# An encoder block on one core: MLP operands made before the norm is known, weight sums added in DRAM, the input in half tiles, products in pairs

## The chip, the cores and the metric

The kernel runs on one core of a Trainium2 chip. The metric is the device time of one execution in microseconds; three runs of the kernel before were timed, and one further execution was profiled. Times below are in microseconds unless marked ns. PE is TensorE, DVE VectorE, ACT ScalarE, POOL GpSimd, SP the engine that issues most DMAs.

## The reference

One encoder layer over 1024 positions with 1024 features, in float32, cut to what matters here:

```python
h = rmsnorm(x, norm_mix_g);  z = h @ w_in                    # split: conv group, latent attention group
y_conv = bg * dwconv_centred(cg * xc, conv_w)                # 512 channels, width 3
y_mla  = mla_attention(q_nope, q_rope, k_nope, k_rope, v)    # 8 heads, softmax over 1024 keys
x = x + concatenate([y_conv, y_mla]) @ w_o

hf = rmsnorm(x, norm_ffn_g)
a = dwconv_centred(hf @ w_up, ffn_conv_w, ffn_conv_b)        # w_up: 1024 x 5632, conv over positions
g, u = split(a)
x = x + (silu(g) * u) @ w_down

gate = sigmoid(rmsnorm(x, ple_norm_g) @ w_ple_gate)
x = x + gate * (p @ w_ple_proj)
out = rmsnorm(x, final_norm_g)
```

`rmsnorm(x, g)` multiplies each position by 1 / sqrt(mean of squares + eps) and each feature by g. The factor of a position is the same for all features, so it can also be applied to the result of a matrix product.

## The kernel before

**Layout.** Activations lie with features on the 128 partitions and positions along the free dimension: eight tiles of 128 x 1024 for x. A float32 product is made from three products of split operands (`gemm`, line 139): each operand is kept as a rounded part ("h", type fp32r) and a remainder ("l"), made by an ACT copy and a DVE or POOL subtraction, and high x high, high x low and low x high are summed in PSUM. A matmul takes a 128 x 128 weight and a 128 x 512 operand.

**Stages in order.** Latent projections; convolution group in four rounds of three products (`unit_gemm`, the result of the third read from PSUM by DVE at line 414); preparation of keys, queries and values; attention; output projection (`out_mla`); the embedding products of p (`embed`) and the MLP's first half in 22 units; down projection in seven groups; gate and final norm.

**Attention.** The loop over `NT` = 64 blocks (8 heads x 8 blocks of 128 queries) issues `scores(i + 2)`, then `transposes(i)`, and every second time `values`. In `scores` DVE takes the maximum (line 511), ACT the exponential, and the scaling by the sum of each row is shared: ACT or DVE take 768 columns, POOL the last 256 (line 521). PE transposes the scaled block (line 534).

**The MLP's first half.** For each unit c (128 gate columns and 128 up columns) the product of the 2 x 2 blocked weight and the 2 x 2 blocked hf is made with seven block products in place of eight (`TERMS`, steps 1 to 7; `BANK` says which PSUM bank each adds into). Its stationary operands are the blocks a11, a12, a22 and four sums s1 to s4 of weight blocks; DVE makes the sums (lines 654 to 657) and the parts are split at lines 645 and 646. The moving operands are blocks b11, b21, b22 of hf and four differences t1 to t4; `up_moving` makes them once for all units: `scaled` (line 723) multiplies x by gain and norm factor, `diff` (line 726) makes differences and remainders, `put` (line 734) the rounded copies. `Unit.step(i)` issues one block product (12 matmuls), and `read` combines the results, then comes the convolution over positions (lines 261 to 263) and the store of the unit's result to `gud`.

**What sets the order.** PE's instructions keep the order of the program (`manual_schedule`). Between `dve_order.enter_context` and `dve_order.close` the same holds for DVE; elsewhere a planner orders the other engines' queues. The norm factors are made by `norm`: `norm_first` (16 small matmuls hung into a `gemm`, line 228), `norm_root` (DVE, lines 233 to 242), `norm_second` (16 small matmuls, line 253). The passage into the MLP runs

```python
    for d in range(6):
        if d == 2:
            norm_first()
        if d == 4:
            norm_second()
        embed(d)
        if d == 2:
            norm_root()
        if d == 4:
            up_moving(rs, lambda: pair.append(up_unit(1, weights1)))
```

and then the first two units' steps in pairs; units 2 to 21 follow one by one. POOL's own DMAs (line 891 loads x for the down projection) use descriptors that software writes; the program reserves `dynamic_dma_scratch_size=1024` bytes for them.

## Time and profile before

| | |
|---|---|
| median of 3 runs | 1356.63 (1356.61 to 1358.47) |
| profiled execution | 1356.78 |
| its span, first to last instruction | 1355.0 |
| mean granted TensorE clock | 0.989 |
| busy: PE, DVE, ACT, POOL | 1323.1, 1006.1, 597.3, 261.3 |
| matmuls | 6354 |
| DMA | 117.38 MB, mean 87 GB/s |

A row of a timeline gives start, duration, engine, line, operation, output <- input, size and count; in brackets stands the idle time before it and what ended that. A row of waits gives who waited for whom: total, times, longest. Rows of windows give the stretch, its length and each engine's busy time with the number of instructions, then the clock, the share of the DMA engines and GB/s.

### The profile page before, as it was taken

How to read it: one execution, taken by the hardware profiler on the slowest of the kernel's cores; microseconds unless marked ns; L12 is line 12 of the kernel's file. 1: busy time of each engine (PE TensorE's matmuls, PEld its weight loads, DVE VectorE, ACT ScalarE, POOL GpSimd, SP SyncE). 2: the span in 40 equal slices, each digit the busy share in tenths (PEclk: the TensorE clock that was granted, in tenths of full speed). 3: DMA queues.
4: the chain of work that ended last, by engine and by line, in shares of the span. 5: the costliest groups of instructions: out<-in, count | busy, mean ns of one | idle time of the engine just before them, and what ended most of it. 6: DMA issues, size and time to landing. Idle time of an engine off the chain costs nothing.

```text
span 1355.0 us, 16462 instructions
## 1 busy us (share of the span) xinstructions
PE 1323.1 (98%) x6354; PEld 1087.7 (80%) x6354; DVE 1006.1 (74%) x1336; ACT 597.3 (44%) x839; POOL 261.3 (19%) x222
## 2 busy tenths in 40 slices
PE   9999999999999999879999999999999999999997
PEld 7877788888888887658888888888877888888897
DVE  7478923799999957988887888888665555557786
ACT  5323422788888834543443444344331111125433
POOL 0286452455555510000000000000010000000000
PEclk9999999999999999979999999999999999999998
DMA  6201134200000254203222222222174222121123
GB/s 215 78 31 47 47 133 148 78 1 17 1 17 1 68 212 171 94 16 124 78 78 78 94 78 78 78 94 74 66 292 165 95 94 94 55 78 55 49 83 111
DMA packets 38894, 117.38 MB, mean 87 GB/s; under 512 B 4256, under 2 KB 9632, under 8 KB 38816
## 3 DMA queue, kind: packets, MB, share of 16 engines
q1 hardware_dynamic: 35824, 107.30, 22.7%
q10 hardware_dynamic: 1840, 4.83, 0.9%
q0 software_dynamic: 1152, 4.19, 0.8%
q8 instruction: 50, 0.82, 0.3%
q14 instruction: 28, 0.23, 0.0%
HBM read 88.00 MB, written 28.31 MB: 86 GB/s over the span
## 4 chain that ended last, share of the span: by engine, by line
PE 85%; DVE 9%; issue 2%; POOL 2%; ACT 1%; DMA 0%; POOLq 0%; SPq 0%; ACTq 0%
PE bk L139 56%; PE big L139 9%; PE small L139 4%; PE small L534 4%; PE small L547 2%; PE big L504 2%; PE big L508 2%; PE big L506 2%; PE small L546 2%; DVE tmp L163 1%; DVE xt L726 1%; DVE tmp L263 1%; DVE tmp L262 1%; DVE b L726 1%; DVE rbc L164 1%
## 5 line engine op out<-in xcount | busy, mean ns | idle before, releaser
L139 PE MATMUL bk<-gu,whi 128*128 128x512 f32 x704 | 194.7, 398 | 2.8 <-DVE x L904 2.2
L139 PE MATMUL bk<-b,wm 128*128 128x512 f32 x792 | 192.8, 396 | 1.7 <-DVE b L726 1.4
L139 PEld LDWEIGHTS bk<-b,wm 128*128 128x128 f32 x792 | 148.5, 188 | 38.7 <-DVE b L726 2.5
L139 PEld LDWEIGHTS bk<-gu,whi 128*128 128x128 f32 x704 | 133.0, 189 | 36.0 <-issue 2.6
L904 DVE TENSOR_TENSOR x<-bk,x 128x512 f32<-128x512 f32 x112 | 71.9, 687 | 89.3 <-PE bk L139 88.8
L139 PE MATMUL bk<-xt,wm 128*128 128x512 f32 x528 | 129.3, 399 | 7.6 <-DVE xt L726 5.4
L128 ACT ACTIVATE whi<-wraw 128x1024 fp32r<-128x1024 f32 (+2 forms) x55 | 51.3, 933 | 187.7 <-PE bk L139 135.4
L139 PEld LDWEIGHTS bk<-xt,wm 128*128 128x128 f32 x528 | 100.8, 192 | 32.6 <-DVE xt L726 7.8
L139 PE MATMUL bk<-b,whi 128*128 128x512 f32 x352 | 112.4, 400 | 3.1 <-DVE b L726 3.1
L646 POOL TENSOR_TENSOR wm<-wraw,wm 128x512 fp32r<-128x512 f32 x22 | 28.8, 1311 | 448.9 <-ACT wm L645 448.9
L139 PE MATMUL bk<-gu,wlo 128*128 128x512 f32 x352 | 111.3, 397 | 0.0
L790 DVE TENSOR_TENSOR tmp<-bk,tmp 128x512 f32<-128x512 f32 x110 | 75.6, 687 | 30.6 <-PE bk L139 30.5
L521 POOL TENSOR_SCALAR tmp<-tmp,sm 128x256 f32<-128x256 f32 x64 | 70.2, 1097 | 101.2 <-DVE sm L514 98.5
L261 ACT ACTIVATE tmp<-tmp,vec 128x1024 f32<-128x1024 f32 x44 | 54.5, 1238 | 71.1 <-DVE tmp L790 71.1
L511 DVE TENSOR_REDUCE mx<-big 128x1 f32<-128x1024 f32 x64 | 78.0, 1218 | 10.3 <-PE big L508 9.8
L537 DVE TENSOR_TENSOR ptl<-small,pth 128x512 fp32r<-128x512 f32 x128 | 83.1, 679 | 1.2 <-ACT pth L536 0.9
L139 PEld LDWEIGHTS bk<-b,whi 128*128 128x128 f32 x352 | 66.9, 190 | 20.2 <-DVE b L726 4.2
L262 DVE SCALAR_TENSOR_TENSOR tmp<-tmp,vec 128x1023 f32<-128x1023 f32 x48 | 63.9, 1331 | 21.6 <-ACT tmp L261 19.2
L139 PEld LDWEIGHTS bk<-gu,wlo 128*128 128x128 f32 x352 | 66.4, 189 | 16.0
L536 ACT CAST pth<-small 128x512 fp32r<-128x512 f32 x128 | 69.0, 591 | 19.8 <-PE small L534 17.3
L513 ACT ACTIVATE tmp<-big,mx 128x1024 f32<-128x1024 f32 x64 | 72.1, 1127 | 5.2 <-DVE sm L514 2.6
L139 PE MATMUL big<-hh,whi 128*128 128x512 f32 x224 | 71.0, 397 | 3.3 <-DVE tmp L414 3.1
(291 smaller groups left out, 2793.6 us busy)
## 6 DMA issues: line engine op xcount, KB each, us to landing
wraw<-in_wun_dram SPq DMA_DIRECT2D x73, 512.0 KB, 3.2
gud<-tmp SPq DMA_DIRECT2D x22, 512.0 KB, 2.6
tmp<-gud SPq DMA_DIRECT2D x22, 512.0 KB, 4.3
wraw<-in_wdn_dram SPq DMA_DIRECT2D x24, 384.0 KB, 3.1
tmp<-in_xT_dram SPq DMA_DIRECT2D x15, 512.0 KB, 4.1
x1d<-tmp SPq DMA_DIRECT2D x8, 512.0 KB, 2.8
xt<-x1d SPq DMA_DIRECT2D x8, 512.0 KB, 6.4
x2d<-xt SPq DMA_DIRECT2D x8, 512.0 KB, 2.7
```

What stands on the lines that cost most here:

```text
L128: act(out=wh, in_=raw, func=AF.Copy)
L139: mm(p, w, x[:, s], start=a, stop=z, skip_group_check=more)
L261: act(out=t, in_=src, func=AF.Identity, scale=vc(w + 1), bias=vc(bias))
L262: stt(out=t[:, 1:S], in0=src[:, 0:S - 1], scalar=vc(w), in1=t[:, 1:S], op0=ALU.mult, op1=ALU.add)
L511: nc.vector.tensor_reduce(m, p, AX.X, ALU.max, negate=True)
L513: act(out=e, in_=p, func=AF.Exp, bias=m, accum_out=su)
L521: nc.gpsimd.tensor_scalar(out=e[:, w:S], in0=e[:, w:S], scalar1=su, scalar2=None, op0=ALU.mult)
L534: nc.tensor.transpose(t[:, k, :], e[:, (g * 4 + k) * P:(g * 4 + k) * P + P], ident)
L536: nc.scalar.copy(out=pth[:, ks, qs], in_=t)
L537: tt(out=ptl[:, ks, qs], in0=t, in1=f(pth)[:, ks, qs], op=ALU.subtract)
L790: add = lambda o, p, q: tt(out=o, in0=p, in1=q, op=ALU.add)
L904: tt(out=x1[d][:, s], in0=q, in1=x1[d][:, s], op=ALU.add)
```

## The change

- **Norm after the products.** x is multiplied by the gain only (`gain`, on ACT), the moving operands are made from that, and `read` multiplies the sums of the products by the norm factor (`rr`). So operands for k = 0 to 2 are made while the output projection still runs. To use adds alone for the weight sums some signs turn: b22 is negated, `add` becomes `diff`, and three convolution weights per unit are negated at the start.
- **Weight sums in DRAM.** s1 to s4 of all 22 units are made during the attention, for pairs of units: a copy DRAM to DRAM issued on SP, then one accumulating DMA on POOL (`accum_op=ALU.add`), two issues per iteration. SP and POOL keep the program's order there. Each unit then loads four sums in place of making them.
- **x in half tiles.** The eight x tiles become sixteen of 128 x 512, loaded, stored and released separately; b21 and b22 take the place of the attention's output tiles, kept until the MLP ends.
- **Products in pairs.** The passage interleaves two embeds, the norm, weights and the steps of units 0 and 1 in a new fixed order, and prepares unit 2 inside it.
- **Convolution group.** ACT copies the third product from PSUM before DVE multiplies it.

```diff
         pb = unit_gemm(U_CONV + 3 * b + 2, hh, hl)
-        tt(out=t1, in0=pb, in1=t1, op=ALU.mult)
+        bc = ft()
+        nc.scalar.copy(out=bc, in_=pb)
+        tt(out=t1, in0=bc, in1=t1, op=ALU.mult)
...
+    wsum = [{m: dram.tile([2, P, 512], F32, name=f"w{m}_{b}") for m in ("s1", "s2", "s3", "s4")} for b in range(NFF // 2)]
+    dmas = []
+    for b0, b1 in ((0, 6), (6, 11)):
+        for m, src in (("s1", A21), ("s2", A11), ("s3", A11), ("s4", A12), ("s1", A22), ("s3", A21), ("s2", "s1"), ("s4", "s2")):
+            for b in range(b0, b1):
+                dmas.append((wsum[b], m, src, b))
+    def add_blocks(n):
+        for _ in range(min(n, len(dmas))):
+            w, m, src, b = dmas.pop(0)
+            o = w[m].rearrange("c p n -> p c n")
+            i = (w[src] if isinstance(src, str) else wup[2 * b:2 * b + 2, src]).rearrange("c p n -> p c n")
+            if m in seen[b]:
+                nc.gpsimd.dma_start(out=o, in_=i, accum_op=ALU.add)
+            else:
+                nc.sync.dma_start(out=o, in_=i)
+            seen[b].add(m)
+    dma_order.enter_context(tc.manual_schedule(engines={mybir.EngineType.Pool, mybir.EngineType.SP}))
     for i in range(NT):
         h = i // 8
+        add_blocks(2)
         if i + 2 < NT:
             scores(i + 2)
...
+    def put_1(k, then=lambda: behind(None)):
+        own = b1 if k < 3 else bt
+        bs[k]["b11"] = put(y1[k][0], own(), own())
+        then()
+        diff(y1[k][0], y1[k][1], y1[k][0])
+        bs[k]["t1"] = put(y1[k][0], own(), own())
+    def put_3(k):
+        diff(y1[k][1], y1[k][1], y2[k][1])
+        bs[k]["t3"] = put(y1[k][1], b1(), b1())
+    def put_t2(k):
+        diff(y2[k][1], y2[k][1], y1[k][0])
+        bs[k]["t2"] = put(y2[k][1], bt(), bt())
+        diff(y2[k][0], y2[k][0], y2[k][1])
...
-            for p, s in pieces(accs[d]):
-                tt(out=x1[d][:, s], in0=p, in1=x1[d][:, s], op=ALU.add)
-            square_acc(ss, x1[d], d == 0, nc.vector)
-        nc.sync.dma_start(out=x2d[d], in_=x1[d]) if d < 7 else None
+            for p, x, s in zip(accs[d] if isinstance(accs[d], list) else halves(accs[d]), x1[d], HALF):
+                tt(out=x, in0=p, in1=x, op=ALU.add)
+                act(out=q[:, s], in_=x, func=AF.Square)
+                nc.sync.dma_start(out=x2d[d][:, s], in_=x)
+            if d:
+                tt(out=ss, in0=ss, in1=q, op=ALU.add)
+            gain(d)
+        if d in (4, 5, 6):
+            put_1(d - 4)
+            put_3(d - 4)
+            behind(None)
...
-        tt(out=s14[:, lo], in0=u[:, lo], in1=u[:, hi], op=ALU.add)
-        tt(out=s23[:, lo], in0=s14[:, lo], in1=g[:, lo], op=ALU.subtract)
-        tt(out=s14[:, hi], in0=g[:, hi], in1=s23[:, lo], op=ALU.subtract)
-        tt(out=s23[:, hi], in0=g[:, lo], in1=u[:, lo], op=ALU.subtract)
+        for to, m in ((s14[:, T1S], "s1"), (s14[:, T2S], "s4"), (s23[:, T1S], "s2"), (s23[:, T2S], "s3")):
+            load(to, wsum[c // 2][m][c % 2])
...
             elif i == 2:
-                nc.scalar.copy(out=g1, in_=p)
+                tt(out=g1, in0=p, in1=rr[:, T1S], op=ALU.mult)
...
+                if len(half) == 2:
+                    tt(out=g2, in0=g2, in1=rr[:, T2S], op=ALU.mult)
+                    finish(gate)
             else:
-                add(u1, p, u1)
+                diff(u1, u1, p)
+                tt(out=au, in0=au, in1=rr, op=ALU.mult)
+                finish(up)
...
+    embed(0)
     for j in range(2):
         embed_weights(j)
-    for d in range(6):
...
+    put_1(3, lambda: put_b21(2))
+    embed(1, norm_first)
+    norm_root()
+    put_b21(3)
+    for k in range(4):
+        put_b22(k)
+    embed(2)
+    norm_second()
+    embed(3)
+    for i in range(2):
+        nc.scalar.copy(out=rr[:, HALF[i]], in_=rs[i])
+    u1 = up_unit(1, weights, post[1])
+    put_3(3)
+    behind(None)
+    weights.pop(0)()
+    weights.pop(0)()
+    for k in range(4):
+        put_t2(k)
+    for k in (0, 3, 1, 2):
+        put_t4(k)
+    behind(None)
+    for d in range(4, NC_):
         embed(d)
+    for i in (1, 5):
+        for unit in (u0, u1):
+            unit.step(i)
...
+    for unit in (u0, u1):
+        unit.step(2)
+    u2 = up_unit(2, weights)
...
+    for i in (3, 6):
+        for unit in (u0, u1):
+            unit.step(i)
...
+    u0.step(7)
+    u1.step(7)
+    post[0].pop(0)()
+    u0.step(4)
...
+    u1.step(4)
     dve_order.close()
```

More of the change, by code (lines that the diff above doesn't have):

```diff
@@ L620, in tile_block, with behind, diff, put @@
     dve_order = ExitStack()
+    low = [None]
+    bs = [{} for _ in range(4)]
+    y1, y2 = x1[0:4], x1[4:8]
+    def behind(fn):
+        if low[0]:
+            low[0]()
+        low[0] = fn
+    def diff(o, p, q):
+        tt(out=o, in0=p, in1=q, op=ALU.subtract)
+    def put(src, h, z, sign=1.0):
+        if sign > 0:
+            nc.scalar.copy(out=h, in_=src)
+            behind(lambda: diff(z, src, f(h)))
+        else:
+            act(out=h, in_=src, func=AF.Copy, scale=sign)
+            behind(lambda: stt(out=z, in0=src, scalar=sign, in1=f(h), op0=ALU.mult, op1=ALU.subtract))
+        return h, z
+    def gain(c):
+        for x in x1[c]:
+            act(out=x, in_=x, func=AF.Copy, scale=vc(V_FFN + c))
+    def put_1(k, then=lambda: behind(None)):
[7 more added lines that the diff above has]
+        bs[k]["t3"] = put(y1[k][1], b1(), b1())
+    def put_b21(k):
+        bs[k]["b21"] = put(y2[k][0], b2s[k][0][:, T1S], b2s[k][1][:, T1S])
+    def put_b22(k):
+        bs[k]["b22"] = put(y2[k][1], b2s[k][0][:, T2S], b2s[k][1][:, T2S], -1.0)
+    def put_t2(k):
+        diff(y2[k][1], y2[k][1], y1[k][0])
+        bs[k]["t2"] = put(y2[k][1], bt(), bt())
+        diff(y2[k][0], y2[k][0], y2[k][1])
+    def put_t4(k):
+        own = bt if k < 2 else b1
+        bs[k]["t4"] = put(y2[k][0], own(), own())
     for d in range(NC_):
@@ L633, in tile_block, with stationary @@
             wj.append(load_unit(wun[U_PROJ]))
-    y_done()
+    b2s = [[yp.tile([P, S], FR, name=f"y{m}{k}") for m in ("mh", "ml")] for k in range(4)]
     T1S, T2S = HALF
-    def stationary(g, u, n, mid, mk, later):
-        lo, hi = slice(0, n), slice(n, 2 * n)
+    def stationary(g, u, s14, s23, later):
         a = {}
+        w2 = lambda m: wp.tile([P, S], FR, name=m)
+        mid = lambda n: sp.tile([P, n * 512], FR, name=f"wm{n}", bufs=6 if n == 2 else 4)
         def put(names, src, h, z, eng):
@@ L779, in embed @@
             gemm(acc, w[0][:, c], w[1][:, c], ph[k][0], ph[k][1], k == 0, k == 1)
+            if k == 0 and between:
+                between()
         t = ft()
@@ new lines, in finish, with gate, up @@
+        def finish(fn):
+            if post is None:
+                fn()
+            else:
+                post.append(fn)
+        def gate():
+            tpool[0] = tmpb
+            t = conv3(ag, V_FW + 6 * c, V_FB + 2 * c)
+            act(out=t, in_=t, func=AF.Silu)
+            out_.append(t)
+        def up():
+            tpool[0] = tmpb
+            t = conv3(au, V_FW + 6 * c + 3, V_FB + 2 * c + 1)
+            tt(out=t, in0=out_[0], in1=t, op=ALU.mult)
+            nc.sync.dma_start(out=gud[c], in_=t)
@@ new lines, in up_unit @@
+        return Unit(a, bs, read)
+    post = [], []
+    u0 = up_unit(0, None, post[0])
+    weights = []
+    dve_order.enter_context(tc.manual_schedule(engines={mybir.EngineType.DVE}))
+    sq, sh = ft(), halves(ft(FR))
+    for p, x, s in zip(accs[7], x1[7], HALF):
+        tt(out=x, in0=p, in1=x, op=ALU.add)
+        act(out=sq[:, s], in_=x, func=AF.Square)
+        nc.sync.dma_start(out=x2d[7][:, s], in_=x)
+    gain(7)
+    for k in range(2):
+        put_b21(k)
+    for h, z, s in zip(sh, sl, HALF):
@@ L1067 @@
     us += units_dk(w_o[512:1024], 2)
-    for c in range(NFF):
-        for o in (0, NFF * P):
-            us.append(unit(w_up[:, o + c * P:o + c * P + P]))
+    wup = w_up.reshape(2, 4, P, 2, NFF, P).transpose(4, 3, 0, 2, 1, 5).reshape(NFF, 4, P, 512)
     dn = []
```

196 lines of the change are left out of this document (72 added, 124 removed).

## The prediction

> **What bounds the kernel now.** I read the page first, then busy time by stage, then the engines one by one in the stage that stands out.
>
> ```profile
> PE 1323.1 (98%) x6354; PEld 1087.7 (80%) x6354; DVE 1006.1 (74%) x1336; ACT 597.3 (44%) x839; POOL 261.3 (19%) x222
> PE   9999999999999999879999999999999999999997
> PEclk9999999999999999979999999999999999999998
> PE 85%; DVE 9%; issue 2%; POOL 2%; ACT 1%; DMA 0%; POOLq 0%; SPq 0%; ACTq 0%
> ```
> TensorE is busy 98% of the span, and the change leaves its number of large matmuls alone. Only its idle time can be won, and that is gathered in slices 16 and 17. In windows by stage (PE, weight load, DVE, ACT, POOL busy, then clock, DMA share, GB/s):
>
> ```profile
> 67.80:169.40 101.60, 98.48 (x420) 78.30 (x420) 85.22 (x65) 35.05 (x40) 65.04 (x24) 1.00 0.12 42
> 247.10:470.50 223.40, 221.85 (x1450) 195.82 (x1448) 204.36 (x343) 184.80 (x331) 120.97 (x138) 1.00 0.04 15
> 488.80:522.60 33.80, 32.51 (x139) 25.60 (x138) 24.81 (x24) 12.94 (x14) 1.31 (x1) 1.00 0.51 187
> 522.60:609.30 86.70, 73.39 (x298) 55.47 (x297) 74.64 (x113) 44.60 (x64) 2.60 (x2) 0.90 0.25 91
> 609.30:643.20 33.90, 33.90 (x148) 27.43 (x147) 29.22 (x31) 13.52 (x17) 2.84 (x2) 1.00 0.34 124
> ```
> They are the convolution, the attention, the output projection, the passage into the MLP, and one steady MLP unit. In the passage DVE is busy 74.6 of 86.7 us and the granted clock falls to 0.90; before and after it PE is full.
>
> ```profile
> 597.53 5.75 PE L139 MATMUL bk<-b,wm 128*128 128x512 f32 x24
> 603.12 2.90 PE L139 MATMUL bk<-xt,wm 128*128 128x512 f32 x12
> 529.34 0.39 PE L139 MATMUL bk<-tmp,whi 128*128 128x512 f32 x1
> 532.88 0.70 PE L139 MATMUL bk<-tmp,whi 128*128 128x512 f32 x2
> 523.99 0.96 PE L139 MATMUL bk<-tmp,whi 128*128 128x512 f32 x3 [0.91 <-DVE xt L824]
> 583.14 1.65 PE L139 MATMUL bk<-xt,wm 128*128 128x512 f32 x3 [2.88 <-DVE xt L726]
> PE bk L139 <- DVE xt L726: 5.4, 4, 2.9
> PE bk L139 <- DVE b L726: 4.5, 4, 2.1
> ```
> The first two rows give the pace: 24 products in 603.12 - 597.53 = 5.59 us, 0.233 each. By the code the passage holds 8 embeds of 12 and two units of 84, 264 products, 61.5 us. The third and fourth rows enclose eight products and sixteen small ones of the norm: 3.54 us, 1.7 more than eight alone; there are two such batches, 3.4. So 64.9 us of work take 86.7, and **21.8 us are lost**: single waits like that of 583.14, on the operands of line 726, and the slow clock after them. That is what there is to win here.
>
> **The change part by part.**
>
> *The passage.* Today `scaled` (line 723) needs the norm, and every operand is made behind it.
>
> ```profile
> 522.64 1.29 DVE L824 TENSOR_TENSOR xt<-small,xt 128x512 f32<-128x512 f32 x2 [1.73 <-PE small L139]
> 528.02 0.69 DVE L829 TENSOR_TENSOR xt<-tmp 128x512 fp32r<-128x512 f32 x1
> 533.05 0.17 DVE L233 TENSOR_SCALAR nv<-bk 128x8 f32<-128x8 f32 x1 [3.13 <-PE bk L228]
> 536.66 0.17 DVE L242 TENSOR_TENSOR nyl<-ny,nyh 128x8 fp32r<-128x8 f32 x1
> 522.60:609.30 86.70, 11.46 (x16) 0.90 0.25 91
> 522.60:609.30 86.70, 28.02 (x40) 0.90 0.25 91
> 586.01 2.50 DVE L726 TENSOR_TENSOR xt<-xt 128x512 fp32r<-128x512 f32 x4
> 588.42 1.22 DVE L646 TENSOR_TENSOR wm<-s,wm 128x1024 fp32r<-128x1024 f32 x1
> ```
> The two window rows are lines 723 and 726 alone. Four half tiles take 588.42 - 586.01 = 2.41 us, 0.60 each; a full tile takes 1.2. Taken from DVE in the passage: the 16 scalings, 11.5; of line 726 all but 29 half tiles by the new code (four b21, four b22, three of `put_1(3)`, two of `put_3(3)`, sixteen of t2 and t4), 28.0 - 17.4 = 10.6; twelve sums of weight halves for units 0 to 2, 7.2. Added: products with `rr`, two halves and a full tile per unit, 2.4 each, 4.8. DVE comes to 74.6 - 11.5 - 10.6 - 7.2 + 4.8 = 50.1 us, against 64.9 of PE. DVE no longer bounds, and the order leaves room: eight embeds stand ahead of the first product, t2 is wanted only in the fifth pair of products, t4 in the last.
>
> What is late next is the norm. Its sums' split ends at 528.0 + 0.7 today; the small products move from the third embed to the second half of the second, that is to 524.0 + 2.8 + 1.4 = 528.2, and DVE has b21 and a weight remainder to fit in besides: PE waits 0 to 2.2, I take 1.4. `norm_root` lasts 536.83 - 533.05 = 3.8, and only one embed (2.8) and one product lie between: 0.8. The wait at 523.99 stays, 0.9. In DVE's fixed order the remainder of unit 1's second sums waits for a `wm2` buffer that unit 0's fourth pair frees, and reads stand behind it: 0 to 3, I take 1.2, since two further pairs of 5.6 us cover most. Left of 21.8: 4.3. **-17.5**; the bounds are -20.9 (only the wait at 523.99 left) and -10 (about half of today's waits stay).
>
> *Ahead of the passage.* Operands of k = 0 to 2 are made here: 15 half tiles on DVE, 9.0, less four sums, 2.4, so 24.8 becomes 31.4 of 33.8 us. ACT gets 14 gains and 9 copies.
>
> ```profile
> 572.75 0.62 ACT L734 CAST xt<-xt 128x512 fp32r<-128x512 f32 x1
> 573.27 0.62 ACT L734 CAST b<-xt 128x512 fp32r<-128x512 f32 x1
> PE big L139 <- ACT whi L128: 0.7, 1, 0.7
> PE big L139 <- DVE wlo L129: 0.6, 1, 0.6
> ```
> At 0.52 each these are 12 us, ACT 24.9 of 33.8. It fits, but the two small waits above, on the last weights of the projection, can grow by what stands in front in these queues: 0 to 4 us, I take +0.8, a little over one instruction. The x half tiles double 8 loads and 8 stores on SP, of 256 KB each; SP waits for nothing late here, so nothing is added.
>
> *Convolution.* ACT copies the third product out (line 414).
>
> ```profile
> PE big L139 <- DVE tmp L414: 3.1, 3, 1.6
> ```
> ACT is busy 35 of 101.6 us there, so the bank comes free about one ACT copy after the product instead of after DVE's queue: between 0 and -3.1, I take **-2**.
>
> *Attention.* 44 copies on SP and 44 adds on POOL, two an iteration: 12 iterations of copies, 12 of adds, then 10 and 10. SP and POOL take a fixed order. SP's copies wait for nothing and only the small weight loads of the queries stand behind them: nothing. The adds are the open price; no row of this trace adds in DRAM.
>
> ```profile
> L511 DVE TENSOR_REDUCE mx<-big x64: 1204/1215/1226, 238.2 to 469.3; 128x1 f32<-128x1024 f32 x64
> POOL tmp L521 <- DVE sm L514: 98.5, 61, 8.2
> 329.10 1.27 POOL L521 TENSOR_SCALAR tmp<-tmp,sm 128x256 f32<-128x256 f32 x1 [1.31 <-DVE sm L514]
> 331.60 1.04 PE L534 MATMUL small<-ident,tmp 128*128 128x128 f32 x8
> 997.80 3.89 POOL L891 DMA_DIRECT2D x<-x2d  x7 [33.25 <-PE bk L139]
> 1003.14 0.54 POOL L891 DMA_DIRECT2D x<-x2d  x1 [1.45 <-issue]
> DMA to landing us min/median/max: 5.0/9.7/16.1
> 1007.00:1010.00 3.00, 3.00 (x15) 2.40 (x14) 0.66 (x1) 1.05 (x1) 0.00 (x0) 1.00 1.02 414
> wraw<-in_wun_dram SPq DMA_DIRECT2D x73, 512.0 KB, 3.2
> ```
> An iteration lasts (469.3 - 238.2) / 63 = 3.67 us. POOL works 121.0 of 223.4 us, 1.99 an iteration; two issues at the 0.53 of line 891 make 3.05. An add has twice the rows of that transfer (256 of 2 KB), so an issue may take 1.06: then 4.11, and 22 iterations lose 0.44 each, 9.7. Engines at a share of 1.02 move 414 GB/s, so 0.524 MB take 1.27 us, and two 2.5 of 3.67, while the DMA share is 0.04 now. Bounds: 0, if an add moves like the transfers of line 891, and +135 (second rival). Nothing below 0, as PE is full there. Of what waits behind POOL: the scaling of the scores' last quarter ends at 330.4 and PE reads it at 331.6, so only 1.2 us of lateness are free. I take **+2**, near the lower end, since the nearest rows (POOL's own 512 KB transfers) fit an iteration twice; the high end stays in the range.
>
> *Steady MLP.* Sums leave DVE (4 x 0.6), products with `rr` come (2.4): 29.2 of 33.9 stays; ACT loses one copy. Loads grow from 1.05 to 1.84 MB per unit, by the 414 GB/s above 1.9 us of transfer in 33.9, ahead of time: 0. If the load of `s14`, with its one buffer, came late, each unit would pay it, but it is free once split. *Ends.* One small DVE instruction at the start, +0.2; later release of the right side before the down projection, 0 to +2, taken 0, as its first tiles wait for `gud` loads too.
>
> Sum on the profiled execution, 1356.78 (span 1355.0 and 1.8 around it; 0.15 above the median of 1356.63): 1356.8 - 17.5 + 0.8 - 2 + 2 + 0.2 = **1340**.
>
> **The rivals.**
>
> *Adds flow at half speed.* If each add reads two streams, it takes 2.53 us, two 5.07 in 3.67. Twelve iterations then owe 60.8 - 44.0, ten 50.7 - 36.7. POOL pauses before its eighth transfer, 5.3 us after the first, when the first has landed (5.0), so some seven may be outstanding, or about three adds; these (7.6 us) and the 1.2 come off each group: 8.0 + 5.2 = 13, in place of the 2: **1351**. For it: the rows of line 891 show that the queue fills. Against it: nothing here reads twice.
> The Trainium skill ("Collectives: The Full Stack", The bandwidth ceiling) says that an adding transfer runs at half the rate of a copy because it needs two source reads; no run here shows it yet, and by it the sum would be this rival's. The Trainium skill ("DMA: Bandwidth & Descriptors", Terms) calls a descriptor a 16-byte struct, written for POOL's transfers into rings in SBUF; with the 1024 bytes that the kernel reserves that agrees with the pause after seven.
>
> *POOL stands still for each add (slower).* If only one add fits in the queue, or the next waits on a sum not yet landed, each costs POOL its issue and its landing, 0.53 + 3.2 (a plain 512 KB load) to 0.53 + 3.2 + 1.27 = 5.0 us, where the pace allows 3.67 / 2 = 1.83. POOL's work between is a quarter of the scores, without which PE's transposes wait: 44 x 1.9 = 83 to 44 x 3.1 = 137, less 2 of cushion: **1420 to 1475**, and 1375 if half overlaps. It decides from 1.83 + 20 / 44 = 2.3 us an add. For it: 1.2 us of slack, a full PE. Against: POOL is idle 46% of the attention, DMA 96%.
>
> *DVE and ACT still bound the passage.* Queues in fixed order, ACT with some 28 us of copies in the embeds' 26: half of today's waits stay, -10 for -17.5: **1348**.
>
> *The change does not do what it says*, the adds being right but the operands still late: within 1354 to 1359. Against it: no operand has the norm in it any more.
>
> **How the numbers follow.** Forecast 1334 to 1345: 0.42. Adds at half speed, 1346 to 1356: 0.14. DVE and ACT, 1345 to 1351: 0.10. POOL standing still, 1360 to 1475: 0.34. Repeats differ by 0.1%, so 0.2% (2.7 us, 1353.9 to 1359.3) is what can be told from no change. Faster is 0.42 + 0.10 + most of 0.14, 0.60; same 0.06; slower 0.34. From 1332 to 1410 lie the first three and some 0.13 of the last, 0.79; the likeliest alone has 1334 to 1345.
>
> **What would show it.** Right: in the passage PE busy within 5 us of its length at a clock of 1.00, the waits on line 726 gone, first MLP product some 30 us after the projection; in the attention the iteration still 3.67 us and no PE wait on POOL. Wrong: PE waiting for `tmp` scaled by POOL, an iteration of 5 us or more where POOL issues adds, POOL idle on "issue" or on a DMA; that alone turns the sign.

## The result, and the profile after

The changed kernel takes 1580.89 us (median of 4 runs, 1574.65 to 1581.83) against 1356.72 for the kernel before: ratio 1.1637, 95% interval 1.1612 to 1.1663, 224 us slower. The forecast was 1340, within 1332 to 1410. Both the sign and the range were wrong.

First the page of the kernel after: busy time by engine, four rows of the 40 slices (tenths; here a slice is 39.5 us), and the shares of the chain that ended last.

```profile
PE 1378.4 (87%) x6354; PEld 1131.3 (72%) x6354; DVE 1018.4 (65%) x1309; ACT 607.1 (38%) x850; POOL 312.1 (20%) x266
PE   6699997984547742999899999999999899999998
...
PEclk8899999996668865999999999999999999999999
DMA  9511149225551356135514333333334532212113
...
PE 67%; issue 12%; POOL 7%; DMA 6%; DVE 6%; ACT 1%; SPq 1%; POOLq 0%; DVEq 0%; ACTq 0%
```

The number of matmuls is the same, but PE is busy 87% of the span where it was 98%. There are three holes: slice 1 and 2, slice 7, and slices 9 to 16. In the first and the seventh the DMA row reads 9. In the third it doesn't, and the chain now holds 12% of "issue" and 7% of POOL. PE's own waits, and one of POOL's (who waited for whom: total, times, longest):

```profile
PE small L543 <- POOL tmp L530: 107.9, 19, 7.7
PE small L144 <- POOL wlo L134: 30.3, 3, 21.2
PE big L144 <- ACT hh L278: 24.2, 2, 12.7
PE big L513 <- DVE tmp L499: 9.4, 1, 9.4
...
POOL ws L602 <- issue: 123.0, 34, 5.0
```

Line 530 is POOL's quarter of the scores and line 134 the low part of the query weights: both belong to the attention. Line 602 is the add in DRAM. Before, PE had no such wait on POOL. The waits on `hh` and on line 499 lie ahead of the attention, where x is loaded. The groups of the row maximum (one per attention block, so first and last start mark the attention), of the copies (line 604) and of the adds:

```profile
L520 DVE TENSOR_REDUCE mx<-big x64: 1206/1223/1225, 279.2 to 697.4; 128x1 f32<-128x1024 f32 x64
...
L604 SPq DMA_DIRECT2D ws<-in_wup_dram x44: 552/557/1212, 5.9 to 269.9; - x44
...
DMA to landing us min/median/max: 5.7/11.6/14.0
...
L602 POOL DMA_DIRECT2D ws<-in_wup_dram x22: 1135/1202/1436, 342.8 to 577.9; - x22
```

The copies stand in the loop of the attention in the program, yet the first was issued at 5.9 us and the last at 269.9, before the attention began. The windows show what that does (stretch, length, busy time of PE, weight load, DVE, ACT, POOL, then clock, DMA share, GB/s):

```profile
0.00:39.50 39.50, 25.92 (x87) 18.98 (x88) 15.46 (x35) 8.85 (x9) 0.19 (x4) 0.83 0.98 324
236.80:276.20 39.40, 29.80 (x130) 23.89 (x128) 12.49 (x15) 8.25 (x13) 6.29 (x4) 0.95 1.03 348
342.00:697.00 355.00, 220.55 (x1148) 189.10 (x1147) 166.30 (x272) 147.23 (x260) 145.28 (x154) 0.77 0.42 72
751.80:825.01 73.21, 68.63 (x297) 55.50 (x296) 49.58 (x79) 35.89 (x56) 2.56 (x2) 0.95 0.37 126
```

The first two windows are full of DMA (0.98 and 1.03), and PE stands idle for a third and a quarter of them. The third is the attention's stretch with adds: PE busy 220.6 of 355 us, clock 0.77, DMA share only 0.42. The last is the passage into the MLP, 73.2 us where it was 86.7.

Split at the first and last row maximum, at the first and last work of the passage, and at the down projection's entry, the 223.5 us of span are:

| stage | before | after | difference | forecast |
|---|---|---|---|---|
| start to first row maximum | 238.2 | 279.2 | +41.0 | +0.2 - 2 |
| attention, first to last row maximum | 231.1 | 418.2 | +187.1 | +2 |
| to the passage (its first embed) | 53.3 | 54.4 | +1.1 | +0.8 |
| passage | 86.7 | 73.2 | -13.5 | -17.5 |
| units 2 to 21 | 389.4 | 389.8 | +0.4 | 0 |
| down projection to the end | 356.3 | 363.7 | +7.4 | 0 |

Within the third stretch POOL's timeline shows the pace of the adds (start, duration; in brackets the idle time before and what ended it):

```profile
361.32 1.16 POOL L602 DMA_DIRECT2D ws<-in_wup_dram  x1 [4.67 <-issue]
362.06 1.39 POOL L530 TENSOR_SCALAR tmp<-tmp,sm 128x256 f32<-128x256 f32 x1
367.23 1.44 POOL L602 DMA_DIRECT2D ws<-in_wup_dram  x1 [3.77 <-issue]
373.15 1.15 POOL L602 DMA_DIRECT2D ws<-in_wup_dram  x1 [4.49 <-issue]
```

One add every 5.9 us; its bar is 1.2 us long, and ahead of it POOL is idle for 3.8 to 4.7 us, waiting for nothing that the profile names. With two adds an iteration, an iteration can't be shorter than about 12 us; it was 3.67.

### The profile page after: what moved, and what is told of

It reads as the page before. It is cut to its first block, busy times and chain, and to the rows that moved or that the text cites. A ratio compares the mean times of both kernels' runs of the same rounds, so it can differ in the third digit from the quotient of the medians.

```text
span 1578.5 us, 16743 instructions
## 1 busy us (share of the span) xinstructions
PE 1378.4 (87%) x6354; PEld 1131.3 (72%) x6354; DVE 1018.4 (65%) x1309; ACT 607.1 (38%) x850; POOL 312.1 (20%) x266
## 3 DMA queue, kind: packets, MB, share of 16 engines
q0 software_dynamic: 13120, 27.27, 9.7%
## 4 chain that ended last, share of the span: by engine, by line
PE 67%; issue 12%; POOL 7%; DMA 6%; DVE 6%; ACT 1%; SPq 1%; POOLq 0%; DVEq 0%; ACTq 0%
PE bk L144 49%; PE big L144 9%; DMA ws<-in_wup_dram 4%; POOL ws L602 3%; PE small L144 2%; POOL tmp L530 2%; DMA tmp<-in_xT_dram 2%; PE small L543 1%; DVE mx L520 1%; PE big L513 1%; PE big L517 1%; PE big L515 1%; PE small L556 1%; PE small L555 1%; DVE ptl L546 1%
## 5 line engine op out<-in xcount | busy, mean ns | idle before, releaser
L543 PE MATMUL small<-ident,tmp 128*128 128x128 f32 x512 | 78.7, 295 | 109.4 <-POOL tmp L530 107.9
L543 PEld LDWEIGHTS small<-ident,tmp 128*128 128x128 f32 x512 | 65.3, 153 | 125.7 <-POOL tmp L530 113.4
L144 PE MATMUL bk<-b,wm 128*128 128x512 f32 x594 | 149.2, 396 | 0.0
L144 PEld LDWEIGHTS bk<-b,wm 128*128 128x128 f32 x594 | 111.6, 188 | 26.5
L144 PE MATMUL bk<-xt,wm 128*128 128x512 f32 x462 | 116.0, 390 | 0.0
L681 DVE TENSOR_TENSOR tmp<-tmp,bk 128x512 f32<-128x512 f32 x110 | 75.2, 685 | 44.9 <-PE bk L144 40.2
L144 PEld LDWEIGHTS bk<-xt,wm 128*128 128x128 f32 x462 | 86.7, 188 | 19.3
L144 PE MATMUL big<-hh,whi 128*128 128x512 f32 x224 | 73.1, 409 | 24.3 <-ACT hh L278 24.2
L530 POOL TENSOR_SCALAR tmp<-tmp,sm 128x256 f32<-128x256 f32 x64 | 75.6, 1196 | 88.4 <-DVE sm L523 86.2
## 6 DMA issues: line engine op xcount, KB each, us to landing
ws<-in_wup_dram SPq DMA_DIRECT2D x44, 512.0 KB, 11.6
```

The costliest lines, as they stand in the source:

```text
L144: mm(p, w, x[:, s], start=a, stop=z, skip_group_check=more)
L530: nc.gpsimd.tensor_scalar(out=e[:, w:S], in0=e[:, w:S], scalar1=su, scalar2=None, op0=ALU.mult)
L543: nc.tensor.transpose(t[:, k, :], e[:, (g * 4 + k) * P:(g * 4 + k) * P + P], ident)
L681: tt(out=o, in0=p, in1=q, op=ALU.subtract)
```

## The experiments

Three theories were on the table for the large term: POOL stands still for the adds (the prediction's second rival), the adds take bandwidth, and the written order of POOL and SP costs by itself. The small terms came along. For each run below, "first" and "last" are the start of the first and last row maximum. Before, after, e1, e5, e6, e7 and e11 were timed 4 to 10 times, and the time is the median; the others were run once. The stages of a run come from its one profiled execution.

| run | first | attention | last maximum to the end | time, us |
|---|---|---|---|---|
| before | 238.2 | 231.1 | 885.7 | 1356.72 |
| after | 279.2 | 418.2 | 881.1 | 1580.89 |
| e1: sums on DVE | 238.5 | 252.6 | 881.1 | 1373.28 |
| e2: copies alone | 277.7 | 255.1 | 879.9 | 1414.43 |
| e3: adds of 256 KB | 276.3 | 341.4 | 882.0 | 1501.47 |
| e4: those in rows of 8 KB | 278.6 | 282.0 | 878.1 | 1440.44 |
| e5: e1, planner's order | 239.8 | 231.1 | 884.2 | 1357.06 |
| e6: e5, other last unit | 239.7 | 231.1 | 881.9 | 1353.62 |
| e7: e6, norm later | 239.9 | 231.1 | 881.0 | 1353.50 |
| e8: before, POOL in written order | 238.5 | 253.0 | 884.3 | 1377.73 |
| e9: before, adds in the units | 257.2 | 231.1 | 885.4 | 1375.62 |
| e10: after, SP's order from earlier | 278.9 | 435.4 | 878.3 | 1594.39 |
| e11: e7, two waits less | 236.4 | 231.1 | 877.4 | 1347.60 |
| e12: e5 and copies behind values | 239.5 | 231.2 | 886.2 | 1358.69 |
| e13: e5 and 29 single adds | 236.5 | 231.2 | 885.8 | 1355.32 |
| e14: e5 and 30 adds in pairs | 238.3 | 276.1 | 888.7 | 1404.94 |
| e15: e14, copies in place of adds | 238.1 | 231.4 | 882.5 | 1353.76 |

**Everything but the DRAM sums (e1).** The four sums of a unit are made on DVE again, from the same blocks, and no copies or adds are issued.

```diff
-        add_blocks(2)
...
+        def sums():
+            for o, p, q in ((s14[:, T1S], u[:, T1S], u[:, T2S]), (s23[:, T1S], s14[:, T1S], g[:, T1S]),
+                            (s14[:, T2S], g[:, T2S], s23[:, T1S]), (s23[:, T2S], g[:, T1S], u[:, T1S])):
+                tt(out=o, in0=p, in1=q, op=ALU.add)
+            put(["s1", "s4"], s14, mid(2), mid(2), nc.vector)
```

> The changed kernel with the weight sums back on DVE (four 128x512 adds per unit, as before the change) and no copies or adds in DRAM; all else of the change stays. Theory (the DRAM copies and adds are the whole loss, the rest of the change is a small gain): the 41 us ahead of the attention and the 187 us in it vanish, the passage keeps most of its 13.4 us gain, the entry into the down projection keeps its 7.4 us loss: 1356.7 - 13.4 + 1.0 + 0.4 + 7.4 = 1352, or up to 1357 if the eight sums of units 0 and 1 cost the passage 5 us again. Rival (the fixed order of POOL, or holding both conv and attention in new buffers, is what slows the attention): the attention stays above 250 us and the time above 1380.

Measured 1373.28, ratio 1.0115 (1.0098 to 1.0132), 16 to 21 us more than expected. Behind the attention it runs as the changed kernel does (881.1 both), so the sums made in DRAM bought nothing that sums on DVE don't give. The surprise is in the attention. The groups and PE's waits of e1:

```profile
L520 DVE TENSOR_REDUCE mx<-big x64: 1206/1218/1226, 238.5 to 491.1; 128x1 f32<-128x1024 f32 x64
...
PE small L144 <- POOL wlo L134: 14.8, 3, 5.6
```

Without a single added DMA the attention lasts 252.6 us, 21.5 more than before, and PE waits for the query weights' low part, which POOL makes. That leads to e8.

**POOL's order alone, on the kernel before (e8).**

```diff
+    dma_order.enter_context(tc.manual_schedule(engines={mybir.EngineType.Pool}))
     for i in range(NT):
...
+    dma_order.close()
```

> The kernel before, with POOL alone kept in the program's order in the attention loop, nothing else changed. Theory 'the written order of POOL holds back the low parts of the next head's query weights, which the planner had moved ahead': attention 231.1 + 15 to 22, that is 246 to 253 us, total 1372 to 1378, and PE waits of 3 to 8 us on wlo. Rival 'it is SP's order, which lets the weights be loaded later': attention within 3 us of 231, total 1355 to 1359.

The row maximum and PE's wait in e8, then the low parts that POOL makes (first and last start), in the kernel before and in e8:

```profile
L511 DVE TENSOR_REDUCE mx<-big x64: 1203/1216/1226, 238.5 to 491.5; 128x1 f32<-128x1024 f32 x64
...
PE small L139 <- POOL wlo L129: 14.8, 3, 5.6
...
L129 POOL TENSOR_TENSOR wlo<-wraw,whi x20: 1284/2406/3384, 44.0 to 324.6; 128x1024 fp32r<-128x1024 f32 x16, 128x512 fp32r<-128x512 f32 x4
...
L129 POOL TENSOR_TENSOR wlo<-wraw,whi x20: 1261/2400/3380, 44.4 to 421.7; 128x1024 fp32r<-128x1024 f32 x16, 128x512 fp32r<-128x512 f32 x4
```

253.0 us and the very same row of waits as in e1. Before, the planner had POOL make the low parts ahead of time, the last at 324.6 us; in the program's order they come behind scalings that wait for DVE, the last at 421.7. POOL's order alone costs 21.9 us, as much as e1's 21.5; SP's order adds nothing to it. The reverse test is e5: e1 without the written order.

> The changed kernel with the sums on DVE (as in e1) and without the written order of POOL and SP in the attention, so that the planner orders these two engines again. Theory 'the written order costs the attention 21.5 us by itself' (e1's attention 252.6 us against 231.1 before): attention 231 to 233 us, the wait of PE on POOL's low parts of the query weights (14.8 us in e1) gone, total 1373.3 - 21.5 = 1352. Rival 'e1's attention is longer because of the loads of x in half tiles or another edit beside the attention': attention stays at 250 or more, total 1370 or more.

The attention is back at 231.1, as expected. The total is 1357.06 (ratio 0.9998, 0.9989 to 1.0007) and not 1352: 1.3 us came at the start (see "The ends" below) and 3.1 behind the attention, which wasn't followed further. So without DRAM sums and written order the change gains and loses the same amount.

**The copies (e2, e10, e12).** In e2 the adds are left out and the copies stay.

> The changed kernel with the 44 adds left out (the units load the first copies in place of the sums, so the results are other numbers); the 44 copies stay. Theory (two separate costs: copies that the planner sends off at the start and before the attention cost 41 us, adds cost 187 in the attention): attention back at 231 us, first maximum still near 279 us, total 1581 - 187 = 1394. Rival (the 41 us come from something else, or the copies slow the attention too): first maximum near 238 us, or an attention above 240 us.

1414.43: of the 41.0 us ahead of the attention the copies alone make 277.7 - 238.5 = 39.2, and in the attention only 2.5. Where they stand in time matters, or their number does; e10 was to tell.

```diff
+    sp_order = ExitStack()
+    sp_order.enter_context(tc.manual_schedule(engines={mybir.EngineType.SP}))
     out_conv(0, [0, 1, 2])
```

> The changed kernel with SP's written order begun at the first product behind the convolution (out_conv) and not only at the attention loop, so that the planner can't move the 44 copies to the program's start; the adds as they were. Theory 'the 41 us ahead of the attention are the copies' rows that go in front of the loads of xT': the first row maximum at 238 to 242 instead of 279.2, attention 418 to 430, total 1538 to 1552. Rival 'the copies cost the same wherever they stand': the attention takes the 41 on, total 1575 to 1585.

A miss, 1594.39. The groups and PE's waits of e10:

```profile
L520 DVE TENSOR_REDUCE mx<-big x64: 1204/1224/1226, 278.9 to 714.3; 128x1 f32<-128x1024 f32 x64
...
PE big L144 <- ACT whi L133: 23.4, 4, 10.9
```

The copies did go to the attention (285.8 to 356.9), but the same 41 us came back for another reason: SP's written order puts weight loads behind stores of x that wait for DVE (97.0 us in eight waits from 180 to 290 us), and PE waits for ACT's `whi`. The edit changed two things, so it told nothing on the copies. e12 holds each copy back by data alone: a DMA of 1 KB from the attention's output goes into its target first.

```diff
+            nc.sync.dma_start(out=w[m][0, 0:1, 0:256], in_=f(YH[h // 2])[h % 2 * 64:h % 2 * 64 + 1, j % 4 * 256:j % 4 * 256 + 256])
+            nc.sync.dma_start(out=w[m].rearrange("c p n -> p c n"), in_=wup[2 * b:2 * b + 2, src].rearrange("c p n -> p c n"))
```

> e5 (sums on DVE, POOL and SP in the planner's order) with the 44 copies of the change put into DRAM tiles that nobody reads, one in each attention iteration from the fifth on. Ahead of each a DMA writes 1 KB of that iteration's attention output into the copy's target, so the planner can't issue the copy before the attention has come so far. Theory 'the copies' 39 us ahead of the attention are their place at the program's start, where xT is being loaded; in the attention they are nearly free': first row maximum at 239 to 241, attention 231 to 235, total 1357 to 1362. Rival 'each copy takes the memory for its 1.3 us or more wherever it stands': attention 250 or more, total 1375 to 1400.

```profile
L520 DVE TENSOR_REDUCE mx<-big x64: 1202/1216/1226, 239.5 to 470.7; 128x1 f32<-128x1024 f32 x64
```

The same 44 copies cost nothing in the attention, and the start is e5's; the total, 1358.69, is 1.6 above e5's, but inside the range of e5's ten runs (1354.46 to 1358.75). What cost 39 us was their place in front of the loads of x.

**The adds (e3, e4, e9, e13 to e15).** First their shape: e3 splits each add into two of 256 KB, and e4 lets a row be 8 KB long.

```diff
-                nc.gpsimd.dma_start(out=o, in_=i, accum_op=ALU.add)
+                for c in range(2):
+                    nc.gpsimd.dma_start(out=o[:, c], in_=i[:, c], accum_op=ALU.add, max_dma_last_dim=8192)   # e3: 2048
```

> The changed kernel with each 512 KB add issued as two of 256 KB, one per unit, rows of 2 KB, at the same places: 88 adds. Theory (POOL's descriptor queue holds one 512 KB add at a time, since an add reads two streams: some 33 of 64 entries per DMA engine; so POOL waits 4.7 us for the landing of each): two or three halves may be under way, POOL's pauses shrink and a 512 KB pair costs 3.2 to 4.5 us in place of 6.1: attention 290 to 350 us (now 418), total 1455 to 1515. Rival (the DMA engines' rate for adds is the limit, or an add's completion): unchanged at 6.1 us a pair or more, total 1570 to 1620, since POOL issues twice as often.

> As the 256 KB adds, but with rows of 8 KB: two rows per DMA engine in place of eight. Theory (number of queue entries decides): at least six halves may be under way, POOL pauses only for its issues and for sums that have not landed: attention 250 to 300 us, total 1415 to 1465. Rival (the engines' rate of adding decides): 3.2 us of all 16 engines per 512 KB as now, attention 290 us or more and no better than with rows of 2 KB.

The page's row of POOL's DMA queue (packets, MB, share of the 16 engines) in e3 with POOL's first adds there, then the same row of e4:

```profile
q0 software_dynamic: 13824, 27.27, 10.8%
...
339.81 2.76 POOL L603 DMA_DIRECT2D ws<-in_wup_dram  x3
344.02 0.83 POOL L603 DMA_DIRECT2D ws<-in_wup_dram  x1 [1.46 <-issue]
...
q0 software_dynamic: 5376, 27.27, 9.1%
```

Both runs came out inside the ranges of their theories. The bytes are the same three times, 27.27 MB. Over e2's 255.1 us the adds cost 163.1 in the changed kernel, 86.3 in e3, and 26.9 in e4, whose adds make a third of e3's packets (4224 against 12672, without the 1152 that the queue has before the change). So it is not the bytes, nor the packets alone, as e3 has more of them than the changed kernel (11968). In e3 three of the smaller adds go in behind one another, and the fourth waits. In e4 no add waits on "issue"; what remains there is POOL's own time for 88 issues of 0.8 us and more (POOL is busy 191.1 us of the attention, 124.4 in e2). But neither run rules out that the memory or the DMA engines set the price. e9 moves 40 adds of the full size to where POOL has next to nothing to do, behind the store of each unit, on the kernel before.

```diff
+                if c < 20:
+                    for k in range(2):
+                        nc.gpsimd.dma_start(out=wsum[k].rearrange("c p n -> p c n"),
+                                            in_=gud[c].rearrange("p (c n) -> p c n", c=2), accum_op=ALU.add)
```

> The kernel before with 40 adds in DRAM of the change's kind (512 KB, 256 rows of 2 KB, POOL's queue, two at a time) put where POOL has next to nothing to do: behind the store of gud of each of the units 0 to 19 of the up-projection, into two DRAM tiles that nobody reads. Theory 'what an add costs is POOL's time, which the attention needs': the units stay at their 389.4 us for 20 of them within 2 us, total 1356 to 1361, each add landing 5 to 7 us after its issue. Rival 'what an add costs is the memory's bandwidth or the DMA engines, some 3.2 us of all 16 for each': the weights' loads come late, PE waits on DMA or on ACT's wm, and the total is 1370 or more.

Its groups, PE's waits, its DMA issues (KB each, median us to landing), the window from 10 to 20 us and SP's load of x there:

```profile
L511 DVE TENSOR_REDUCE mx<-big x64: 1202/1215/1226, 257.2 to 488.3; 128x1 f32<-128x1024 f32 x64
...
PE big L139 <- ACT hh L271: 14.8, 1, 14.8
...
wsum<-gud POOLq DMA_DIRECT2D x40, 512.0 KB, 6.2
...
10.00:20.00 10.00, 9.02 (x38) 6.91 (x37) 3.00 (x6) 0.41 (x1) 0.00 (x0) 1.00 0.13 53
...
12.88 10.09 SPq L316 DMA_DIRECT2D tmp<-in_xT_dram  x1
```

1375.62, above the expected range, for a reason that has nothing to do with the adds: the two targets are filled by two plain 512 KB copies, which the planner put at the program's start, and the first row maximum came 19 us later. Like e2's copies they stand in front of the loads of x, but they don't fill the DMA engines: the share is only 0.13, that of two engines out of 16, and SP needs 10.1 us to issue the load behind them. In the trace the two copies add four 4-byte records, two each, to the hardware queue q1 (3956 against 3952 before), where a 512 KB add has 16; they seem to have run on two engines each. From the last row maximum to the end it takes 885.4 us, before 885.7: the 40 adds cost nothing there. That speaks against the memory and the DMA engines and for POOL's time; e13 shows the same inside the attention.

The next question was whether an add holds POOL through its own transfer, or only until the one before it has left the queue. e13 and e14 have e5's attention with the same adds, single in every second iteration or two together in every fourth, held in place by a 1 KB write as in e12.

```diff
+        if i >= 6 and i % 2 == 0:        # e14: i % 4 == 2
+            for _ in range(1):           # e14: 2
+                add_block(i // 2 - 1)
```

> e5 (sums on DVE, POOL and SP in the planner's order) with 29 adds of the change's kind (512 KB, 256 rows of 2 KB) into DRAM tiles that nobody reads, a single one in every second attention iteration (some 7.2 us apart), each behind a 1 KB write of the attention's output into its target, so that it can't be issued earlier. Theory 'an add holds POOL for its issue of 1.2 us; what costs 3.7 us apiece in the changed kernel is that the next add, right behind it, waits in POOL until the one before has landed': attention 231 to 250 us, total 1357 to 1376, no POOL idle of 5 us on the adds' line. Rival 'each add holds POOL through its whole transfer': 29 x 3.7 = 107 more, attention 320 to 345.

> The same with 30 adds, two behind one another in every fourth attention iteration. Theory 'the second add waits in POOL for the first to land': POOL idle of some 5 us ahead of the second of each pair (15 x 5 = 75 us), attention longer than e13's by 15 x 3 to 15 x 6 = 45 to 90 us. Rival 'each add holds POOL through its whole transfer': attention as in e13 within 10 us.

The groups, a row of POOL's timeline and the adds' landing in e13:

```profile
L520 DVE TENSOR_REDUCE mx<-big x64: 1202/1215/1226, 236.5 to 467.7; 128x1 f32<-128x1024 f32 x64
...
310.83 1.23 POOL L601 DMA_DIRECT2D wsum<-in_wup_dram  x1 [0.98 <-DMA wsum<-ymh]
...
DMA to landing us min/median/max: 5.5/5.7/8.8
```

and in e14 the groups, PE's waits, POOL's DMA queue and two adds:

```profile
L520 DVE TENSOR_REDUCE mx<-big x64: 1206/1224/1226, 238.3 to 514.4; 128x1 f32<-128x1024 f32 x64
...
PE small L543 <- POOL tmp L530: 34.5, 13, 4.0
...
q0 software_dynamic: 9312, 19.93, 7.8%
...
313.08 1.22 POOL L601 DMA_DIRECT2D wsum<-in_wup_dram  x1 [0.94 <-DMA wsum<-ymh]
319.07 1.15 POOL L601 DMA_DIRECT2D wsum<-in_wup_dram  x1 [4.77 <-issue]
```

29 single adds: attention 231.2 us, no cost at all. 30 in pairs: 276.1, 45 more, 3.0 a pair. The first of a pair goes in at once; ahead of the second POOL stands idle 4.8 us here, 67.6 us over the 15 pairs, put down to "issue" or to whichever engine happened to come last. It does nothing else then, though scalings of the scores are behind it and PE waits for them. So an add costs POOL its 1.2 us, and the next add right behind it costs the rest of the first one's landing.

What remained was why seven of POOL's plain 512 KB transfers go in without a wait (line 891 before the change) and only one add: the rows (256 against 128) or the adding.

```diff
-            nc.gpsimd.dma_start(out=o, in_=i, accum_op=ALU.add)
+            nc.gpsimd.dma_start(out=o, in_=i)
```

> e14 with the 30 adds of POOL made plain copies of the same shape (512 KB, 256 rows of 2 KB, POOL's queue, in pairs in every fourth iteration), nothing else changed. Theory 'the rows fill the queue, whether they add or not': POOL idle some 3 us or more ahead of the second of each pair, attention 255 to 276 us. Rival 'an adding transfer takes more of the queue than a copy, of which seven with 128 rows went in before the change': no idle time ahead of the second, attention 231 to 236, total 1355 to 1362.

The queue, the groups and a pair in e15:

```profile
q0 software_dynamic: 5472, 19.93, 4.4%
...
L520 DVE TENSOR_REDUCE mx<-big x64: 1204/1215/1226, 238.1 to 469.5; 128x1 f32<-128x1024 f32 x64
...
L601 POOL DMA_DIRECT2D wsum<-in_wup_dram x30: 687/752/920, 275.0 to 483.5; - x30
...
DMA to landing us min/median/max: 3.6/4.1/6.3
...
319.56 1.45 POOL L601 DMA_DIRECT2D wsum<-in_wup_dram  x2
```

No wait between the two, attention 231.4. POOL issues a copy in 0.75 us instead of 1.2, and it lands after 4.1 us instead of 5.7. But the copies did not keep the rows of the adds. A copy makes 144 packets, (5472 - 1152) / 30 (the 1152 are the eight x loads): in the trace 128 of 4 KB and 16 of 4 bytes. An add makes 272, (13120 - 1152) / 44 in the changed kernel: 256 of 2 KB and 16 of 4 bytes. So e15 by itself doesn't tell the rows from the adding. e3 does: its adds of 256 KB have 144 packets too, 12672 / 88, and only three of them go in, where seven transfers of line 891 with 144 packets did. Both count, the adding and the number of rows.

One way of counting fits all of this; it is an estimate from these packets. Shared by 16 engines, an add has 17 packets per engine, one of e3 has 9, one of e4 has 3 and a copy has 9, one of each being the 4-byte end. Let a row of an add take two places in the queue and a row of a copy one: then an add takes 33 places, one of e3 17, one of e4 5 and a copy 9. One add fits and a second (66) doesn't; three of e3 fit (51) and a fourth (68) doesn't; seven copies fit (63) and an eighth (72) doesn't. That makes 63 to 65 places. No run varied the size of the queue.

**The small terms, and a version that beats both (e6, e7, e11).** e6 lets the last unit read the b2 tiles earlier.

```diff
-        for i in (1, 6, 5, 2, 7, 3):
+        for i in (1, 6, 5, 2, 7, 3) if unit is not final_unit[0] else (1, 5, 2, 3, 6, 7):
```

> e5, and the last unit of the up-projection runs its steps in the order 1, 5, 2, 3, 6, 7, 4, so that its readers of the b2 tiles end earlier. Theory 'the entry of the down-projection is 7.4 us later than before since the gu tiles lie over b2 tiles that are freed late': down-projection from its entry 357 to 360 us instead of 363.7, total e5 - 4 to - 7, some 1347. Rival 'the entry waits for the loads of gu whatever is freed': no change to e5 within 1 us.

1353.62 (ratio 0.9968, 0.9959 to 0.9977). The down projection takes 359.1 us instead of e5's 363.1, its entry comes 1.6 later. The mechanism is as expected, the net gain is 3.4, under the expected 4 to 7.

> e6, the second half of the norm one embedding product later (after embed(3) instead of after embed(2)), and the negation of the conv weights made behind the attention instead of at the program's start. Theory: PE's 3.1 us wait on DVE's nyh in the passage goes or shrinks below 1 (with the slower clock that follows it), and the start's +2.2 us goes: e6 - 3 to - 6, some 1341 to 1344, below both kernels. Rival 'the operands become late instead, as rr and t2 to t4 come one embedding later': the wait moves to DVE's operands ahead of unit step 1 and the passage is as long as in e6; total e6 - 2.

1353.50, no gain over e6. The wait on the norm went (it was 1.1 us in e6), but PE's wait for `x` in the down projection grew from 2.2 to 3.5, and the other half of the edit did nothing: the negation, written behind the attention, was still put at the start by the planner. DVE's and PE's timeline of e7:

```profile
4.60 0.20 DVE L629 TENSOR_SCALAR vec<-vec 128x66 f32<-128x66 f32 x1 [3.02 <-DMA vec<-in_vecs_dram]
...
6.24 1.22 PE L142 MATMUL big<-hh,whi 128*128 128x512 f32 x2 [0.83 <-DVE hh L330]
```

e11 puts it on ACT, and the low part of the last projection weights on POOL.

```diff
-    nc.vector.tensor_scalar(out=neg, in0=neg, scalar1=-1.0, scalar2=None, op0=ALU.mult)
+    act(out=neg, in_=neg, func=AF.Copy, scale=-1.0)
...
+        loeng[0] = nc.gpsimd if d == 6 else nc.vector
         out_mla(d, [3] if d < 3 else [0, 1, 2, 3])
```

> e7 with two waits less: the negation of the conv weights on ACT instead of DVE (in e7 the planner still put it at 4.6 us on DVE, ahead of the first hh, and PE's first product came at 6.24 instead of 5.35 us, with a clock below full until 11 us), and the low part of the out-projection's last weights on POOL instead of DVE (PE waits 2.45 us for it in e7). Theory: the first row maximum at 236 to 238 instead of 239.9, the wait at 515.8 below 1.8; total e7 - 2 to - 5, that is 1348.5 to 1351.5. Rival 'another wait takes their place (ACT's start, the product behind)': no change to e7 within 1 us.

```profile
5.28 1.54 PE L142 MATMUL big<-hh,whi 128*128 128x512 f32 x2
...
L518 DVE TENSOR_REDUCE mx<-big x64: 1204/1216/1226, 236.4 to 467.5; 128x1 f32<-128x1024 f32 x64
```

1347.60, ratio 0.9923 (0.9910 to 0.9937): 9.5 us faster than the kernel before, 0.9 below the expected range, and the expected wait of 1.6 us on POOL in place of 2.45. PE's first product comes at 5.28 us and the first maximum 3.5 us earlier than in e7. The change without its sums in DRAM and without the written order is worth having, once these small losses are repaired; the sums in DRAM, as issued here, are not.

## Why the prediction was wrong

**The step that failed: the adds, taken at +2, measured +163.** The prediction set "0, if an add moves like the transfers of line 891" against "+135 (second rival)", and chose the low end since "the nearest rows (POOL's own 512 KB transfers) fit an iteration twice". e15 shows that this would have been right for plain copies of the same bytes. The nearest row was near in bytes, but an add has twice its rows and each takes more of the queue, so one add fills the queue alone. The prediction did ask how many may be outstanding, and counted "about three adds" by their transfer time; it was one. The second rival named the mechanism ("only one add fits in the queue") and priced it at 1.9 to 3.1 an add above the pace; measured 163.1 / 44 = 3.7, as the issue took 1.2 us where the rival had 0.53, and the landing 5.7 where it had 3.2 to 4.5. The clock, 0.77 in the attention's stretch with adds, goes with it. The attention's 187.1 us are made up of 21.5 for the written order (e1 over before), 2.5 for the copies (e2 over e1) and 163.1 for the adds (after over e2).

The rival "adds flow at half speed" was near in the rate and wrong about the price. POOL's queue took 7.8% of the 16 engines' span in e14 (1403.1 us) and 4.4% in e15 (1352.0); less the 0.8% that it has before the change for the x loads, some 10.8 us, an add takes (109.4 - 10.8) / 30 = 3.3 us of all engines and a copy (59.5 - 10.8) / 30 = 1.6. In rows of 8 KB (e4) an add takes 2.7, (130.9 - 10.8) / 44. The Trainium skill ("Collectives: The Full Stack", The bandwidth ceiling) says of a ReduceScatter that it runs at half the rate of an AllGather because its add needs two source reads. These runs are in line with that, 3.3 or 2.7 against 1.6, though no run has adds and copies in the same rows. It isn't what the attention pays, as e9 and e13 show. The Trainium skill ("Perfetto Trace Analysis", DMA Instruction — SWDGE (GPSIMD)) says that the bar of such an instruction ends when its descriptors are written, not when the data has moved. The traces agree: bar 1.2 us, landing 5.7; the full queue shows as idle time ahead of the next bar, put down to "issue" or to the engine that came last.

**Written order of POOL, priced at nothing, measured +21.9 (e8) and +21.5 (e1).** The sentence was "SP and POOL take a fixed order". The prediction asked what stands behind the added DMAs, but not what the planner had been doing with the instructions that the fixed order now holds. The row to look at was in the trace of before: POOL's last `wlo` starts at 324.6 us, less than half way through the attention.

**Copies, "nothing", measured +39.2 ahead of the attention and +2.5 in it (e1, e2).** "SP's copies wait for nothing" was true, and that was the trouble: an instruction that waits for nothing is free to be issued first. A written order of two engines inside a section fixes the sequence of that section, not the time at which it begins. No rival held the copies or the written order, so the result lies even above the second rival's 1475.

**The passage, -17.5, measured -13.5.** DVE at 49.6 us busy (forecast 50.1), no wait on the operands: the mechanism was right. The waits left are 0.91, 0.45 and 3.11 us, together 4.5 where the sum kept 4.3, but that they agree is luck: the split of the norm's sums cost 0.45 (forecast 1.4), the `wm2` buffer nothing (1.2), and the result of `norm_root` 3.11 (0.8). The 0.8 let `norm_root` begin at once; it began 2.4 us after the last of the 16 small products (at 763.70, their end at 761.30), behind the last of six other pieces of work in DVE's fixed order. What the sum left out is the clock behind that wait, 0.76 from 768 to 780 us. Two rows of PE's timeline after: the norm's wait, and one at the down projection's entry.

```profile
767.51 0.44 PE L260 MATMUL bk<-b,nyh 128*128 128x128 f32 x1 [3.11 <-DVE nyh L248]
...
1230.34 0.73 PE L144 MATMUL bk<-gu,whi 128*128 128x512 f32 x2 [3.54 <-ACT gu L274]
```

At a mean clock of 0.95 the passage loses some 3.7 of its 73.2 us beside the waits. 64.9 of work, 4.5 of waits and 3.7 of clock give 73.1.

**The ends.** The down projection, "0 to +2, taken 0", took +7.4: the `gu` tiles lie where b21 and b22 were, and the last unit read those to its end (e6 gives back 4.0 of it behind the entry, which comes 1.6 later). The start, "+0.2" for one small DVE instruction, cost up to 3.5 (e7 against e11): it waits for a DMA, stands ahead of the first operands on DVE, and in e7 PE starts 0.9 later and has the full clock only from 11.0 us by the trace's records, in e11 from 6.9. How much of that is chance isn't settled: with the same instruction in place and the first product at 5.70 us, e13 has the full clock from 6.5 us and its first maximum at 236.5, as early as e11.

**What held.** Convolution -2: with the start repaired, e11's first maximum is 1.8 earlier than before's; PE's waits of 3.1 us for line 414 are gone, and the waits for POOL's `wlo` ahead of the attention have grown from 0.3 to 2.1 us. Ahead of the passage +0.8: +1.1. Steady units 0: +0.4.

The signs named for a wrong forecast, PE waiting for `tmp` scaled by POOL, an iteration of 5 us or more, and POOL idle on "issue", are what the trace after shows: the first and last row of waits, and (697.4 - 279.2) / 63 = 6.6 us an iteration.

## What to carry to other kernels

Before moving work to an engine's DMA queue, ask how many transfers of that very shape the queue holds, and keep two of them further apart than one takes to land, or count the engine as standing still; a copy of the same bytes is no measure for an add. Work that waits for nothing has no place in time, and a scheduler may put it in front of the loads that everything else needs; hold it back by a real dependence. A written order also takes away what the scheduler had been doing for you, so before writing one, look in the trace for the instructions that now run ahead of their place in the program.

## What the runs showed of the hardware

- A single add of 512 KB in DRAM, 256 rows of 2 KB, issued by POOL: 1.2 us of POOL, landing after 5.7 us; the next one right behind it left POOL idle for 4.8 us. A copy of the same bytes, which went as 128 packets of 4 KB: 0.75 us, 4.1 us, and no wait between two. Of adds of 256 KB in rows of 2 KB three went in without a wait. 29 single adds, some 7 us apart, cost an attention that is bound by PE nothing.
- Copies from DRAM to DRAM without a wait, 44 of 512 KB, kept the DMA engines at a share of 0.98 to 1.03 (324 and 348 GB/s) and landed after 11.6 us. In front of the loads of x they cost 39 us, one by one in the attention nothing (e12). Two others at the program's start cost 19 us at a DMA share of only 0.13 (e9).
- With PE's repeated waits (19 for the scaled scores alone, 5.7 us in the mean) the granted clock went down: 0.77 over 355 us of the attention with adds, 1.00 in the same loop of e12 with 44 copies and no adds.
